# Row softmax of 512 MB on one core: the steady part of the unrolled kernel put into a hardware loop with register-based waits

## The chip, the cores and the metric

One core of a Trainium2 chip runs the kernel; the other cores idle. The metric is device time in microseconds (us), the median of several executions.

## The reference, cut to what matters

```python
logits: (16, 256, 32768) float32, temperature = 1.0
scaled = logits / temperature
scaled = scaled - scaled.max(axis=-1, keepdims=True)
e = np.exp(scaled)
out = e / e.sum(axis=-1, keepdims=True)          # float32
```

There are 4096 rows of 32768 numbers: 537 MB are read and 537 MB written. Each byte is moved once in each direction.

## The kernel before: the parts that matter

A row is split into two halves on two partitions, so a *group* is 64 rows on 128 partitions. A group is two *chunks* of 128 x 8192 numbers, 4 MiB each; there are 64 groups and 128 chunks. Six chunk buffers are used in turn. VectorE (DVE) takes each chunk's maximum, ScalarE (ACT) its exponentials and their sum. A few tiny instructions combine the two chunks and the two halves into factors; then DVE scales one half of each chunk and ACT the other. SyncE (SP) issues every load and store. Its main lines, shortened:

```python
xpool = ctx.enter_context(tc.tile_pool(name="x", bufs=6))
...
order = [("L", i) for i in range(6)] + [("S", 0)]         # L: load, S: compute and store
for i in range(1, n_chunks):
    order.append(("S", i))
    if i + 5 < n_chunks:
        order.append(("L", i + 5))                        # into the buffer of chunk i - 1
...
    if g > done:                                          # first chunk of a group
        exps(2 * g); exps(2 * g + 1); factors(g)
    scales(i); store(i)
```

All 128 chunks are unrolled. A scheduler orders DVE and ACT; loads and stores stay in program order.

## Time and profile before

| | before |
|---|---|
| time, median of 4 runs beside the changed kernel | 2494.67 us |
| DMA queue, share of the 16 engines' span | 99.9% |
| bytes moved, rate in the steady part | 1073.76 MB, 433 GB/s |
| DVE busy, ACT busy | 60%, 56% |
| instruction packets (they fetch the program while it runs) | 17 |

The queue row is the one to read: it is full. A busy engine at 60% has nothing to say about the time here. The lines themselves are in the prediction.

### The profile page before, as it was taken

To read this page: it belongs to the slowest core of one execution; us is meant where nothing else is said; L and a number is where in the kernel's file an instruction comes from. 1 tells how busy PE (TensorE), PEld (TensorE's weight loads), DVE (VectorE), ACT (ScalarE), POOL (GpSimd) and SP (SyncE) were. 2 spreads that over 40 slices of the span, in tenths; PEclk is the share of its full clock that TensorE was granted. 3 is DMA by queue.
4 is the path that set the end of the run, shared out by engine and by line. 5 is a ranking of instruction groups with operands and counts; after the bars stand their busy time and mean duration, and the time that the engine had idled before them with its cause. 6 is when DMAs were issued, how large, how long until landed. Compare 5 with 4: busy or idle time off the path is not lost.

```text
span 2493.8 us, 2234 instructions
## 1 busy us (share of the span) xinstructions
DVE 1487.4 (60%) x964; ACT 1405.0 (56%) x455; POOL 0.2 (0%) x4
## 2 busy tenths in 40 slices
DVE  7655565556655566555665566655666566655663
ACT  5665554655556555565555655555546555465553
POOL 0000000000000000000000000000000000000000
DMA  9999999999999999999999999999999999999998
GB/s 412 433 430 432 429 431 432 433 433 434 433 434 432 435 432 435 432 435 431 436 431 435 432 434 433 434 433 433 433 433 433 433 433 434 434 433 434 432 431 368
DMA packets 37745, 1073.90 MB, mean 431 GB/s; under 512 B 4192, under 2 KB 4192, under 8 KB 4192
## 3 DMA queue, kind: packets, MB, share of 16 engines
q1 hardware_dynamic: 37728, 1073.76, 99.9%
q14 instruction: 17, 0.14, 0.0%
HBM read 536.87 MB, written 536.87 MB: 431 GB/s over the span
## 4 chain that ended last, share of the span: by engine, by line
DMA 96%; SPq 1%; ACT 1%; DVE 1%; issue 1%; ACTq 0%
DMA out_dram<-xs 93%; DMA xs<-in_logits_dram 2%; SPq L64 1%; DVE nm L107 1%; ACT xs L163 1%; ACT xs L114 0%; ACTq L224 0%; SPq L75 0%; DVE f L150 0%; ACT ee L131 0%; DVE rS L149 0%; DVE Sh L87 0%; DVE ttj L138 0%; DVE Sh L84 0%; DVE Sh L138 0%
## 5 line engine op out<-in xcount | busy, mean ns | idle before, releaser
L114 ACT ACTIVATE xs<-xs,nm 128x8192 f32<-128x8192 f32 (+1 forms) x130 | 912.1, 7016 | 972.4 <-DVE nm L107 972.4
L107 DVE TENSOR_REDUCE nm<-xs 128x1 f32<-128x8192 f32 (+1 forms) x130 | 1111.6, 8551 | 527.3 <-DMA xs<-in_logits_dram 527.3
L163 ACT ACTIVATE xs<-xs,f 128x4096 f32<-128x4096 f32 (+1 forms) x130 | 468.1, 3648 | 71.4 <-DVE f L150 71.4
L160 DVE TENSOR_SCALAR xs<-xs,f 128x4096 f32<-128x4096 f32 (+1 forms) x130 | 295.7, 2318 | 3.7 <-DVE f L150 1.8
L138 DVE CUSTOM_DVE_ANT_0 ttj<-ee,ssum 128x2 f32<-128x2 f32 x64 | 10.3, 161 | 423.8 <-ACT ee L131 423.8
L114 ACT ACTIVATION_READ_ACCUMULATOR xs<-xs,nm 128x1 f32 x130 | 24.2, 186 | 0.0
L131 ACT ACTIVATE ee<-nm,nMh 128x2 f32<-128x2 f32 x64 | 17.9, 280 | 0.0
L150 DVE TENSOR_SCALAR f<-ee,rS 128x2 f32<-128x2 f32 x64 | 14.6, 229 | 2.2
L149 DVE RECIPROCAL rS<-Sh 128x1 f32<-128x1 f32 x64 | 10.5, 164 | 2.2
L87 DVE TENSOR_TENSOR nMh<-nMh 128x1 f32<-128x1 f32 x64 | 10.2, 160 | 2.2
L87 DVE TENSOR_TENSOR Sh<-Sh 128x1 f32<-128x1 f32 x64 | 10.2, 160 | 2.2
L129 DVE TENSOR_REDUCE nMh<-nm 128x1 f32<-128x2 f32 x64 | 9.9, 155 | 2.2
L84 DVE STREAM_SHUFFLE nMh<-nMh 128x1 f32<-128x1 f32 x64 | 9.7, 151 | 0.0
L84 DVE STREAM_SHUFFLE Sh<-Sh 128x1 f32<-128x1 f32 x64 | 9.7, 151 | 0.0
L114 ACT ACT_TABLE_LOAD x1 | 1.3, 1283 | 12.9 <-DMA xs<-in_logits_dram 12.9
L138 DVE DVE_READ_ACCUMULATOR2_ANT Sh<- 128x1 f32 x64 | 5.3, 84 | 0.0
L84 DVE LOAD_MASK_SELECT Sh<-Sh x64 | 0.9, 14 | 2.8
L84 DVE LOAD_MASK_SELECT nMh<-nMh x64 | 0.9, 14 | 2.7
L210 POOL MEMSET const-bfloat16-1.0<- 128x1 bf16 x1 | 0.1, 102 | 0.0
L210 POOL MEMSET const-uint8-127<- 128x1 uint8 x1 | 0.1, 102 | 0.0
L210 POOL MEMSET const-float32-0.0<- 128x1 f32 x1 | 0.1, 99 | 0.2 <-issue 0.2
L210 POOL MEMSET const-float32-1.0<- 128x1 f32 x1 | 0.1, 99 | 0.0
## 6 DMA issues: line engine op xcount, KB each, us to landing
out_dram<-xs SPq DMA_DIRECT2D x126, 4096.0 KB, 38.2
xs<-in_logits_dram SPq DMA_DIRECT2D x124, 4096.0 KB, 29.0
xs<-in_logits_dram SPq DMA_DIRECT2D x8, 2048.0 KB, 22.3
out_dram<-xs SPq DMA_DIRECT2D x4, 2048.0 KB, 26.7
```

Of the source, the lines that this page charges most:

```text
L64: nc.sync.dma_start(out=xs[:, s : s + n], in_=x[g * P : (g + 1) * P, c * CW + s : c * CW + s + n],)
L84: nc.vector.stream_shuffle(out=v[:, j + 1 : j + 2], in_=v[:, j : j + 1], mask=mask)
L87: nc.vector.tensor_tensor(out=v[:, j + 1 : j + 2], in0=v[:, j : j + 1], in1=v[:, j + 1 : j + 2], op=op,)
L107: nc.vector.tensor_reduce(out=nm[:, k : k + 1], in_=xs[:, s : s + n], axis=X, op=A.max, negate=True)
L114: nc.scalar.activation(out=xs[:, s : s + n], in_=xs[:, s : s + n], func=Exp, bias=nm[:, k : k + 1], scale=inv_t, accum_out=ssum[:, k : k + 1],
L129: nc.vector.tensor_reduce(out=nMh[:, 0:1], in_=nm, axis=X, op=A.min)
L131: nc.scalar.activation(out=ee, in_=nm, func=Exp, bias=nMh[:, n_rounds : n_rounds + 1], scale=-1.0,)
L138: nc.vector.tensor_tensor_reduce(out=ttj, in0=ee, in1=ssum, scale=1.0, scalar=0.0, op0=A.mult, op1=A.add, accum_out=Sh[:, 0:1],)
L149: nc.vector.reciprocal(out=rS, in_=Sh[:, n_rounds : n_rounds + 1])
L150: nc.vector.tensor_scalar_mul(out=f, in0=ee, scalar1=rS)
L160: nc.vector.tensor_scalar_mul(out=xs[:, s : s + cut], in0=xs[:, s : s + cut], scalar1=f[:, k : k + 1])
L163: nc.scalar.activation(out=xs[:, s + cut : s + n], in_=xs[:, s + cut : s + n], func=Copy, scale=f[:, k : k + 1],)
```

## The change

The intent is a short program: 114 of the 128 chunks are handled by 19 turns of a hardware loop whose body holds six chunks, one per buffer, 24 MiB loaded and 24 MiB stored in each turn. A loop of this kind needs no stop between turns: its semaphores are never reset, and every wait in the body compares with a register that is raised in each turn. For that the buffers become fixed tiles, and the engines run in the order in which the program names the work. Six chunks before the loop and eight after it stay unrolled.

```diff
-    xpool = ctx.enter_context(tc.tile_pool(name="x", bufs=_BUFS))
-    spool = ctx.enter_context(tc.tile_pool(name="stats", bufs=3))
+    pool = ctx.enter_context(tc.tile_pool(name="fixed", bufs=1))
+    buf = [pool.tile([P, CW], fp32, tag=f"x{b}", name=f"x{b}") for b in range(_BUFS)]
     ... (three fixed sets of the small tiles)
+    def rows(i, turn, per_turn):
+        g = i // C
+        if turn is None:
+            return slice(g * P, (g + 1) * P)
+        return bass.ds(turn * (per_turn // C * P) + g * P, P)     # address from a register
     ...
+    def step(i, turn=None, per_turn=0):
+        g, c = divmod(i, C)
+        end = turn is None and g == G - 1
+        if c == 0:
+            normalise(g, _END_PIECE if end else _PIECE)   # maxima, exponentials, factors, scaling
+        store(i, _END_DMA if end else CW, turn, per_turn)
+        j = i + _BUFS - 1
+        if i and j < n_chunks:
+            ... load(j, ...)
+    with tc.manual_schedule():
+        for i in range(_BUFS):
+            load(i, _END_DMA if i < C else CW)
+        for i in range(first):                                       # first = 6
+            step(i)
+        with tc.For_i(0, turns, 1, iteration_sync="reg_based") as turn:   # turns = 19
+            for i in range(first, first + per_turn):                  # per_turn = 6
+                step(i, turn, per_turn)
+        for i in range(first + turns * per_turn, n_chunks):           # chunks 120 to 127
+            step(i)
```

More of the change, by code (lines that the diff above doesn't have):

```diff
@@ L12 @@
 _PIECE = 8192
-_LAST_DMA = 4096
+_END_DMA = 4096
+_END_PIECE = 4096
 _DVE_SHARE = 0.5
+_SETS = 3
 @with_exitstack
@@ L45 @@
     n_rounds = _SPLIT.bit_length() - 1
-    xpool = ctx.enter_context(tc.tile_pool(name="x", bufs=_BUFS))
-    spool = ctx.enter_context(tc.tile_pool(name="stats", bufs=3))
-    slots = {}
-    stats = {}
+    K = W // min(_PIECE, _END_PIECE)
+    pool = ctx.enter_context(tc.tile_pool(name="fixed", bufs=1))
+    buf = [
+        pool.tile([P, CW], fp32, tag=f"x{b}", name=f"x{b}") for b in range(_BUFS)
+    ]
+    widths = dict(nm=K, ssum=K, ee=K, f=K, ttj=K, nMh=2, Sh=2, rS=1)
+    stat = [
+        {
+            k: pool.tile([P, w], fp32, tag=f"{k}{s}", name=f"{k}{s}")
+            for k, w in widths.items()
+        }
+        for s in range(_SETS)
+    ]
@@ L52, in spans @@
     def spans(total: int, step: int) -> list[tuple[int, int]]:
         return [(s, min(step, total - s)) for s in range(0, total, step)]
-    def piece(g: int) -> int:
-        return _PIECE if g < G - 1 else min(_PIECE, _LAST_DMA)
-    def load(i: int) -> None:
-        g, c = divmod(i, C)
-        xs = xpool.tile([P, CW], fp32, tag="x", name="xs")
-        slots[i] = xs
-        for s, n in spans(CW, _LAST_DMA if g in (0, G - 1) else CW):
-            tc.keep_in_program_order(
-                nc.sync.dma_start(
-                    out=xs[:, s : s + n],
-                    in_=x[g * P : (g + 1) * P, c * CW + s : c * CW + s + n],
-                )
-            )
@@ L70, in store, with rows @@
-    def store(i: int) -> None:
-        g, c = divmod(i, C)
-        xs = slots.pop(i)
-        for s, n in spans(CW, _LAST_DMA if g == G - 1 else CW):
-            tc.keep_in_program_order(
-                nc.sync.dma_start(
-                    out=o[g * P : (g + 1) * P, c * CW + s : c * CW + s + n],
-                    in_=xs[:, s : s + n],
-                )
+    def rows(i: int, turn, per_turn: int):
+        g = i // C
+        if turn is None:
+            return slice(g * P, (g + 1) * P)
+        return bass.ds(turn * (per_turn // C * P) + g * P, P)
@@ new lines, in load, with store @@
+    def load(i: int, step: int, turn=None, per_turn: int = 0) -> None:
+        c = i % C
+        for s, n in spans(CW, step):
+            nc.sync.dma_start(
+                out=buf[i % _BUFS][:, s : s + n],
+                in_=x[rows(i, turn, per_turn), c * CW + s : c * CW + s + n],
+            )
+    def store(i: int, step: int, turn=None, per_turn: int = 0) -> None:
+        c = i % C
+        for s, n in spans(CW, step):
+            nc.sync.dma_start(
+                out=o[rows(i, turn, per_turn), c * CW + s : c * CW + s + n],
+                in_=buf[i % _BUFS][:, s : s + n],
@@ L92, in combine, with pieces, normalise @@
             )
-    def exps(i: int) -> None:
-        g, c = divmod(i, C)
-        xs = slots[i]
-        ps = spans(CW, piece(g))
-        K = C * len(ps)
-        if c == 0:
-            stats[g] = tuple(
-                spool.tile([P, K], fp32, tag=f"{nm}{K}", name=nm)
-                for nm in ("nm", "ssum", "ee", "f", "ttj")
-            )
-        nm, ssum = stats[g][:2]
-        for j, (s, n) in enumerate(ps):
-            k = c * len(ps) + j
+    def pieces(g: int, step: int):
+        k = 0
+        for c in range(C):
+            xs = buf[(g * C + c) % _BUFS]
+            for s, n in spans(CW, step):
+                yield k, xs[:, s : s + n], n
+                k += 1
+    def normalise(g: int, step: int) -> None:
+        st = stat[g % _SETS]
+        K = W // step
+        nm, ssum, ee, f, ttj = (st[k][:, :K] for k in ("nm", "ssum", "ee", "f", "ttj"))
+        nMh, Sh, rS = st["nMh"], st["Sh"], st["rS"]
+        for k, xc, n in pieces(g, step):
             nc.vector.tensor_reduce(
-                out=nm[:, k : k + 1], in_=xs[:, s : s + n], axis=X, op=A.max, negate=True
+                out=nm[:, k : k + 1], in_=xc, axis=X, op=A.max, negate=True
             )
@@ L114, in exps @@
             nc.scalar.activation(
-                out=xs[:, s : s + n],
-                in_=xs[:, s : s + n],
+                out=xc,
+                in_=xc,
                 func=Exp,
@@ L121, in exps @@
             )
-    def factors(g: int) -> None:
-        nm, ssum, ee, f, ttj = stats[g]
-        nMh = spool.tile([P, 1 + n_rounds], fp32, tag="nMh", name="nMh")
-        Sh = spool.tile([P, 1 + n_rounds], fp32, tag="Sh", name="Sh")
-        rS = spool.tile([P, 1], fp32, tag="rS", name="rS")
-        with tc.high_priority():
-            nc.vector.tensor_reduce(out=nMh[:, 0:1], in_=nm, axis=X, op=A.min)
-            combine(nMh, A.min)
-            nc.scalar.activation(
-                out=ee,
-                in_=nm,
-                func=Exp,
-                bias=nMh[:, n_rounds : n_rounds + 1],
-                scale=-1.0,
-            )
-            nc.vector.tensor_tensor_reduce(
-                out=ttj,
-                in0=ee,
-                in1=ssum,
-                scale=1.0,
-                scalar=0.0,
-                op0=A.mult,
-                op1=A.add,
-                accum_out=Sh[:, 0:1],
-            )
-            combine(Sh, A.add)
-            nc.vector.reciprocal(out=rS, in_=Sh[:, n_rounds : n_rounds + 1])
-            nc.vector.tensor_scalar_mul(out=f, in0=ee, scalar1=rS)
@@ L152, in scales @@
-    def scales(i: int) -> None:
-        g, c = divmod(i, C)
-        xs = slots[i]
-        f = stats[g][3]
-        ps = spans(CW, piece(g))
-        for j, (s, n) in enumerate(ps):
-            k = c * len(ps) + j
+        nc.vector.tensor_reduce(out=nMh[:, 0:1], in_=nm, axis=X, op=A.min)
+        combine(nMh, A.min)
+        nc.scalar.activation(
+            out=ee, in_=nm, func=Exp, bias=nMh[:, n_rounds : n_rounds + 1], scale=-1.0
+        )
+        nc.vector.tensor_tensor_reduce(
+            out=ttj,
+            in0=ee,
+            in1=ssum,
+            scale=1.0,
+            scalar=0.0,
+            op0=A.mult,
+            op1=A.add,
+            accum_out=Sh[:, 0:1],
+        )
@@ L159, in scales @@
+        combine(Sh, A.add)
+        nc.vector.reciprocal(out=rS, in_=Sh[:, n_rounds : n_rounds + 1])
+        nc.vector.tensor_scalar_mul(out=f, in0=ee, scalar1=rS)
+        for k, xc, n in pieces(g, step):
             cut = int(n * _DVE_SHARE) // 512 * 512
             nc.vector.tensor_scalar_mul(
-                out=xs[:, s : s + cut], in0=xs[:, s : s + cut], scalar1=f[:, k : k + 1]
+                out=xc[:, :cut], in0=xc[:, :cut], scalar1=f[:, k : k + 1]
             )
             nc.scalar.activation(
-                out=xs[:, s + cut : s + n],
@@ L165, in scales @@
-                in_=xs[:, s + cut : s + n],
-                func=Copy,
-                scale=f[:, k : k + 1],
-            )
-    order = [("L", i) for i in range(min(_BUFS, n_chunks))] + [("S", 0)]
-    for i in range(1, n_chunks):
-        order.append(("S", i))
-        if i + _BUFS - 1 < n_chunks:
-            order.append(("L", i + _BUFS - 1))
-    nxt = 0
-    done = -1
-    loaded = 0
-    for kind, i in order:
-        if kind == "L":
-            load(i)
-            loaded = i + 1
-        else:
-            g = i // C
-            if g > done:
-                while nxt < (g + 1) * C:
-                    assert nxt < loaded
-                    exps(nxt)
-                    nxt += 1
-                factors(g)
-                done = g
-            scales(i)
-            store(i)
+                out=xc[:, cut:], in_=xc[:, cut:], func=Copy, scale=f[:, k : k + 1]
+            )
@@ new lines, in step @@
+    def step(i: int, turn=None, per_turn: int = 0) -> None:
+        g, c = divmod(i, C)
[5 more added lines that the diff above has]
+        if i and j < n_chunks:
+            end = turn is None and j // C == G - 1
+            load(j, _END_DMA if end else CW, turn, per_turn)
+    per_turn = 6
+    first = per_turn
+    turns = (n_chunks - (_BUFS - 1) - C - first) // per_turn
@@ L197 @@
+    assert turns > 0
+    with tc.manual_schedule():
[8 more added lines that the diff above has]
+            step(i)
 _INS = ['logits', 'temperature']
```

## The prediction

> **What bounds the kernel now.** I read the page from the top: busy shares, the 40 slices, the chain that ended last, then the waits of the DMA queue, then one stretch of the timeline. The first lines are these.
>
> ```profile
> span 2493.8 us, 2234 instructions
> DVE 1487.4 (60%) x964; ACT 1405.0 (56%) x455; POOL 0.2 (0%) x4
> ...
> GB/s 412 433 430 432 429 431 432 433 433 434 433 434 432 435 432 435 432 435 431 436 431 435 432 434 433 434 433 433 433 433 433 433 433 434 434 433 434 432 431 368
> ...
> q1 hardware_dynamic: 37728, 1073.76, 99.9%
> ...
> DMA 96%; SPq 1%; ACT 1%; DVE 1%; issue 1%; ACTq 0%
> ```
>
> Both compute engines are idle 40% of the time, the data queue's packets fill 99.9% of the 16 DMA engines' span, and the rate is flat at about 433 GB/s. The chain of waits is 96% DMA. So the time is bytes over rate: 1073.76 MB / 433.4 GB/s = 2477.5 us, and about 17 us remain for the slower start, and for the tail that shows as 368 in the last slice.
>
> The second question is how much work stands in the queue, because the change touches the waits there. The waits of the queue and the issue table show it.
>
> ```profile
> SPq L64 <- DMA out_dram<-xs: 2246.9, 122, 19.6
> ...
> out_dram<-xs SPq DMA_DIRECT2D x126, 4096.0 KB, 38.2
> xs<-in_logits_dram SPq DMA_DIRECT2D x124, 4096.0 KB, 29.0
> ```
>
> SP waits 122 times, 18.4 us on average, always before a load, for the store that frees its buffer. Call the store of chunk i S(i) and its load L(i). When S(i) has landed, L(i+6) goes out and S(i+2) directly after it. In the queue's timeline these refills stand 19.35 us apart, which is 8.39 MB (one load and one store of 4 MiB) at 433.4 GB/s. A single 4 MiB transfer therefore takes 9.67 us. The latencies fit a first-in first-out queue exactly: two transfers (19.35 us) still stand ahead, so the load lands after three (29.0) and the store after four (38.7, seen 38.2). Every refill finds 19.35 us of transfers in hand.
>
> The third question is how long one group of two chunks takes to compute when nothing overlaps it. This is from the timeline at 1978 us.
>
> ```profile
> 1978.30 8.69 DVE L107 TENSOR_REDUCE nm<-xs 128x1 f32<-128x8192 f32 x1 [8.31 <-DMA xs<-in_logits_dram]
> ...
> 1987.02 7.12 ACT L114 ACTIVATE xs<-xs,nm 128x8192 f32<-128x8192 f32 x1 [9.78 <-DVE nm L107]
> ...
> 1994.14 0.28 ACT L131 ACTIVATE ee<-nm,nMh 128x2 f32<-128x2 f32 x1
> ...
> 1995.24 0.23 DVE L150 TENSOR_SCALAR f<-ee,rS 128x2 f32<-128x2 f32 x1
> 1995.57 7.31 ACT L163 ACTIVATE xs<-xs,f 128x4096 f32<-128x4096 f32 x2 [1.15 <-DVE f L150]
> ```
>
> From the second reduction to the first half of the scaling it takes 1995.57 + 7.31/2 - 1978.30 = 20.9 us; with the first chunk's reduction before it, 20.9 + 8.7 = 29.6 us. A group's share of the queue is 38.7 us, so this is hidden today.
>
> **What the Trainium skill says.** "DMA: Bandwidth & Descriptors", section "Where 436 GB/s comes from", puts the ceiling of the 16 ports at 435.2 GB/s. The 433.4 measured is within half a per cent of it, so there is nothing to win in the steady part. The same page, "Anatomy of one DMA", gives about 2 us fixed per transfer, mostly the receipt of the last bytes, and says that waits happen on the issuing sequencer. The trace agrees: the first 4 MiB is issued from 0.73 us and released its reduction at 12.89, so 12.16 - 9.67 = 2.5 us beyond the transfer. "Runtime: NRT & Kernel Launch", section "Instruction fetch mechanics", warns that a taken branch to a target outside the two pages held makes the engine fetch before it goes on. No trace of the kernel before can show that; it has no loop.
>
> **The change part by part.** I compared the built orders of instructions and semaphores of both kernels.
>
> *Bytes.* None change: the same 264 transfers in the same order of loads and stores. Term: 0.
>
> *Engines in program order.* The scheduler had put the next group's first reduction between this group's exponentials and its factors; now the factors and scaling come first. Per group DVE has 2 x 8.7 + 2 x 2.3 + about 1.5 = 23.5 us of work in 38.7 us. It stays hidden. Term: 0.
>
> *Register arithmetic and the branch.* The loop is 19 turns of 6 chunks (chunks 6 to 119); 6 chunks before it and 8 after it are unrolled. No engine meets a barrier at the end of a turn: each adds to its wait registers and branches. SP branches just after a load, when it would wait some 19 us for the next landing anyway. Term: 0.
>
> *A new wait inside the loop.* With addresses from a register the framework no longer sees that two stores go to different rows. In the loop every store waits until the store before it has landed, the first store of a turn included. So S(i+1) and L(i+6) go out when S(i) lands, and the queue then holds one load, 9.67 us, not 19.35. Less the 2.5 us fixed cost, some 7 us are in hand, and the order of transfers is the same. If no DMA engine runs dry, the term is 0; a store's latency in the table should drop from 38 to about 19 us and a load's stay at 29.
>
> *The end of the loop.* Here something is added once. After the last turn SP waits for every transfer of the loop, then all engines meet at a barrier; only then do DVE and ACT start on chunks 120 and 121, though both landed long before. S(120) is next in SP's order, and L(125) stands behind it although its buffer is free. So the DMA engines idle for: fixed cost of the last landing and of the first new issue 2.5 us (above), barrier about 0.7 us (SP's wait for the others at the start was 0.7 us), compute 29.6 us, issue 0.4 us. Sum **33.2 us**. Nothing can hide it: the queue is the bound, and time lost there is not won back. Following the eight chunks after it by the same durations, S(122) and S(124) are ready before the queue is empty, and the store of chunk 126 comes within about 1 us of its emptying. Term: +33.2 + 1 = 34.
>
> *Instruction fetches.* The 2234 instructions before came in through 17 packets of the instruction queue. The refill intervals are 19.35 us except for one of 20.16, 0.8 us longer, every 16 chunks, and a handful of longer ones in the first 20 chunks; all this excess is about 11 us. A loop may remove part of it. Term, a guess: -3.
>
> Sum: 2494.9 + 34 - 3 = 2526 us, 1.2% longer.
>
> **The rivals.** *A.* The store-to-store wait starves the queue. Against it: 7 us are in hand. For it: the 16 DMA engines do not end together (in the last 14 us the rate falls step by step, so some finish some 10 us before the last), and with a shorter queue the early ones will idle. As long as the slowest never runs dry it alone sets the pace. But if the pace stays at the 19.6 us of the first 20 chunks rather than 19.35, 114 chunks x 0.28 us add 32 us: 2558 us. If every refill exposed the 2.5 us, 114 x 2.5 = 285 us: 2810 us; the queue's arithmetic speaks strongly against that.
>
> *B.* Every turn stalls on an instruction fetch or a hidden drain. The program shows no drain in the body, and the branch has some 19 us of slack; 5 us exposed per turn would be 95 us: 2621 us.
>
> *C.* The end of the loop is hidden after all, because instructions behind the barrier are short or loads run ahead. Then 2490 to 2495 us. Against it: the barrier stands in every engine's order, and the 29.6 us of compute cannot start before it.
>
> **Range and chances.** 2527 us is the sum of the one-time gap and a small gain. Low end 2508: a gap of 25 us and most of the 11 us of excess gone. High end 2553: the gap plus a good part of rival A. The 2% line lies at 2544.8; the gap alone does not cross it, so it takes rival A or B to cross. I give that 16%. Faster by over 2% would need 1073.76 MB in 2445 - 17 = 2428 us, 442 GB/s, above anything the slices show: 1%.
>
> **What would show each step.** In the changed profile: one hole of about 33 us in the DMA row near 2385 us (the loads of chunks 126 and 127 wait today for the store of chunk 121 until 2415 us), with DVE's first reduction after it released by the barrier and not by a load; otherwise 433 GB/s per slice; store latency near 19 us and load latency near 29; SP's waits on a store's landing moved from the loads to the stores; fewer instruction packets. The prediction is wrong if the slices in the loop lie below 430 GB/s (A), if a dip comes every 116 us (B), or if no hole is there (C).

## The result, and the profile after

The changed kernel takes **2531.05 us** (median of 4 runs, 2530.07 to 2532.89) against 2494.67 us (4 runs). The ratio is 1.0147, with a 95% interval of 1.0129 to 1.0165. Ratios here are the mean time of one kernel's runs over the mean of the other's in the same rounds, so not quite the ratio of the medians. The profiled executions have spans of 2529.0 and 2493.8 us: **35.2 us** are to be found.

The page of the changed kernel, the lines that answer to those shown of before:

```profile
span 2529.0 us, 4017 instructions
DVE 1486.7 (59%) x964; ACT 1405.5 (56%) x455; POOL 0.2 (0%) x4
...
GB/s 415 431 399 421 433 431 430 431 434 433 433 432 434 433 433 433 434 433 434 432 434 433 434 432 434 433 434 432 434 433 434 432 434 433 434 432 434 300 314 416
...
q1 hardware_dynamic: 37728, 1073.76, 98.6%
q14 instruction: 2, 0.02, 0.0%
...
DVE 3%; ACT 1%; ACTq 0%; issue 0%
...
out_dram<-x SPq DMA_DIRECT2D x126, 4096.0 KB, 19.2
x<-in_logits_dram SPq DMA_DIRECT2D x124, 4096.0 KB, 28.3
```

The bytes and the compute are those of before. Most of the 1800 instructions more are register arithmetic, counted in every turn. Slices 5 to 37 are as fast as before. Two places are not: slices 3 and 4 (399, 421), and slices 38 and 39 (300, 314). The chain that ended last names only some 5% of the span: it could be followed back to a barrier and no further, so here it does not say what bounds the kernel.

The second place is where the loop ends. The timeline there (start, duration, engine, line, operation; L83 is the store, L75 the load, L115 the maximum, L122 the exponential, L153 ACT's scaling):

```profile
2358.41 0.34 SPq L83 DMA_DIRECT2D out_dram<-x  x1
2358.97 0.35 SPq L75 DMA_DIRECT2D x<-in_logits_dram  x1
2388.08 17.28 DVE L115 TENSOR_REDUCE nm<-x 128x1 f32<-128x8192 f32 x2 [75.64 <-PEq L213]
...
2405.39 7.12 ACT L122 ACTIVATE x<-x,nm 128x8192 f32<-128x8192 f32 x1 [1.38 <-DVE nm L115]
...
2413.94 7.31 ACT L153 ACTIVATE x<-x,f 128x4096 f32<-128x4096 f32 x2 [1.15 <-DVE f L147]
2417.67 0.34 SPq L83 DMA_DIRECT2D out_dram<-x  x1
```

SP issues the loop's last load at 2358.97 us. The waits of the queue tell that it then stands for that load:

```profile
SPq L178 <- DMA x<-in_logits_dram: 27.6, 1, 27.6
```

So the loop is drained at about 2387 us. DVE starts at 2388.08 us, after 75.64 us of idleness; "PEq" is only the last engine to come to the barrier, not work of TensorE. The compute up to the next store takes 2417.67 - 2388.08 = 29.6 us. What the DMA engines did meanwhile (stretches of 10 us, the first of 20; the last two numbers are the share of the 16 DMA engines and GB/s):

```profile
2360.00:2380.00 20.00, 0.00 (x0) 0.00 (x0) 0.00 (x0) 1.00 1.00 433
2380.00:2390.00 10.00, 1.92 (x1) 0.00 (x0) 0.00 (x0) 1.00 0.31 134
2390.00:2400.00 10.00, 10.00 (x2) 3.20 (x1) 0.00 (x0) 1.00 0.00 0
2400.00:2410.00 10.00, 5.82 (x5) 8.62 (x3) 0.00 (x0) 1.00 0.00 0
2410.00:2420.00 10.00, 6.99 (x10) 8.85 (x5) 0.00 (x0) 1.00 0.25 105
```

That is the hole of the prediction. The queue was empty while DVE and ACT worked, and before that DVE and ACT had idled while the queue worked.

The first place is where the loop is entered:

```profile
141.25 0.34 SPq L75 DMA_DIRECT2D x<-in_logits_dram  x1
142.02 17.28 DVE L115 TENSOR_REDUCE nm<-x 128x1 f32<-128x8192 f32 x2 [36.84 <-SPq L178]
...
171.67 0.35 SPq L83 DMA_DIRECT2D out_dram<-x  x1
```

DVE had finished the group before at 105 us, and chunk 6, its next, should have been there (loaded from 72.05 us; a load takes 28.3 us). It waits 36.84 us for "SPq L178", the line of the loop itself, and goes on just after SP has issued its last load ahead of the loop. The reason is not in the trace; this is how I read the built program: the waits in the loop use semaphores of the loop's own, and each engine gives its own semaphores their starting count where it stands in its program ahead of the loop. The counts for the loads are SP's, and SP comes to that place only when it has issued the unrolled part's last load, at 141.25 us. So the store of chunk 6 goes out at 171.67 us, when three queued transfers (29.0 us) have run dry. The DMA engines from 164 to 176 us, in slices of 0.3 us (each digit is their busy share in tenths):

```profile
DMA  2997299729992020002000000000900092009500
```

A ledger follows from the queue's timelines. It gives the time at which a load is issued in the changed kernel, less the time of the same load in the kernel before (in the last row, the spans):

| load of chunk | changed less before, us | run with the compute ahead (below) less before, us |
|---|---|---|
| 10 (before the loop is entered) | +0.7 | +0.9 |
| 15 | +5.4 | +2.0 |
| 25 | +6.4 | +0.4 |
| 65 | +4.5 | -1.3 |
| 124 (last of the loop) | +1.7 | -4.2 |
| end | +35.2 | 0.0 |

The entry costs 4.7 us by load 15 and 5.7 us by load 25; from there to load 124 the changed kernel gains 4.7 us on the kernel before; the exit costs 33.5 us. The gain is in the refill intervals. Before, from load 25 on, seven late ones of 20.16 us stand among those of 19.35. Each of the seven holds one instruction packet; the other ten of the 17 packets go with no late interval after load 25. In the changed kernel there are 2 packets, none between 110 and 2440 us, and no such interval. So the late intervals go with fetches; that the fetch makes them late is not shown. From load 28 to 124 the sum of what exceeds 19.355 us falls from 4.7 to 0.7 us.

### The profile page after: what moved, and what is told of

The parts are those of the page before. It is cut to its first block, busy times and chain, and to the rows that moved or that the text cites. A ratio compares the mean times of both kernels' runs of the same rounds, so it can differ in the third digit from the quotient of the medians.

```text
span 2529.0 us, 4017 instructions
## 1 busy us (share of the span) xinstructions
DVE 1486.7 (59%) x964; ACT 1405.5 (56%) x455; POOL 0.2 (0%) x4
## 5 line engine op out<-in xcount | busy, mean ns | idle before, releaser
L122 ACT ACTIVATE x<-x,nm 128x8192 f32<-128x8192 f32 (+1 forms) x130 | 912.1, 7016 | 1017.5 <-DVE nm L115 678.2
L115 DVE TENSOR_REDUCE nm<-x 128x1 f32<-128x8192 f32 (+1 forms) x130 | 1110.5, 8550 | 559.8 <-DMA x<-in_logits_dram 447.4
L153 ACT ACTIVATE x<-x,f 128x4096 f32<-128x4096 f32 (+1 forms) x130 | 468.1, 3649 | 73.4 <-DVE f L147 73.4
L150 DVE TENSOR_SCALAR x<-x,f 128x4096 f32<-128x4096 f32 (+1 forms) x130 | 295.7, 2318 | 2.3
L122 ACT ACTIVATION_READ_ACCUMULATOR x<-x,nm 128x1 f32 x130 | 24.2, 186 | 0.0
## 6 DMA issues: line engine op xcount, KB each, us to landing
out_dram<-x SPq DMA_DIRECT2D x126, 4096.0 KB, 19.2
x<-in_logits_dram SPq DMA_DIRECT2D x124, 4096.0 KB, 28.3
```

What stands on the lines that cost most here:

```text
L115: nc.vector.tensor_reduce(out=nm[:, k : k + 1], in_=xc, axis=X, op=A.max, negate=True)
L122: nc.scalar.activation(out=xc, in_=xc, func=Exp, bias=nm[:, k : k + 1], scale=inv_t, accum_out=ssum[:, k : k + 1],)
L150: nc.vector.tensor_scalar_mul(out=xc[:, :cut], in0=xc[:, :cut], scalar1=f[:, k : k + 1])
L153: nc.scalar.activation(out=xc[:, cut:], in_=xc[:, cut:], func=Copy, scale=f[:, k : k + 1])
```

## The experiments

My theory was: one hole at the exit, made of drain and compute; one small hole at the entry; a small gain from fetches; and nothing from the turns or from the stores that wait for one another. The rivals were a cost of each turn, a cost of the store-to-store wait, and a cost of program order. Twelve kernels ran, all with correct results. The kernel before, run beside them, had medians of 2494.2 to 2494.6 us.

**Program order and fixed buffers without a loop.**

```diff
-        for i in range(first):
-            step(i)
-        with tc.For_i(...) as turn: ...
-        for i in range(first + turns * per_turn, n_chunks):
+        for i in range(n_chunks):
             step(i)
```

> The change without its loop: fixed buffers, engines in program order, all 128 chunks unrolled. Theory (the loss is one gap where the loop is left, one small gap where it is entered, less instruction fetches that the loop saves): none of these three is here, so 2494 to 2496 us, within 3 us of the kernel before, with 433 GB/s in every slice, refills of 19.35 us with the 0.8 us longer ones still there, and no hole. Rival (program order itself or the fixed buffers cost time, because factors and scaling now stand before the next reduction): 2505 us or more.

Measured: 2494.92 us, ratio 1.0004 (0.999 to 1.0017). There are 17 instruction packets again, and the intervals of 20.15 to 20.17 us are back. Program order and fixed buffers cost nothing; the 36 us need the loop or what comes with it.

**Compute a group ahead of the loop's boundary.** The computing of group g+1 moves from just before its own stores to just after the stores of group g.

```diff
-        if c == 0:
-            normalise(g, _END_PIECE if end else _PIECE)
         store(i, _END_DMA if end else CW, turn, per_turn)
         ... load(j, ...)
+        if c == C - 1 and g + 1 < G:
+            last = turn is None and g + 1 == G - 1
+            normalise(g + 1, _END_PIECE if last else _PIECE)
 ...
+        normalise(0, _PIECE)
         for i in range(first):
             step(i)
```

> The changed kernel with one thing moved: a group is computed after the stores of the group before it, not directly before its own stores, so chunks 120 and 121 are computed before the loop is left, and 6 and 7 before it is entered. Store-to-store waits, turns, barrier and drain stay as they were. Theory: the hole at the exit shrinks from 33 us by the 29.6 us of compute to about 3.6 us (fixed cost 2.5, barrier 0.7, issue 0.4), the hole at the entry (about 4 us, from DVE idle 36.8 us until SP reached the loop) is gone, the saved fetches stay: 2490 to 2495 us, as fast as the kernel before or a little faster. Rival (the loss is in the turns, or in the wait of a store for the store before it): 2520 us or more, as both are still there.

Measured: 2495.39 us, ratio 1.0007 (0.9994 to 1.0021). The turns, the store-to-store waits, the drain and the barrier are all still there, and the loss is gone. The timeline at the exit:

```profile
2353.14 0.35 SPq L75 DMA_DIRECT2D x<-in_logits_dram  x1
2382.29 17.28 DVE L115 TENSOR_REDUCE nm<-x 128x1 f32<-128x8192 f32 x2 [36.95 <-PEq L215]
2382.31 0.34 SPq L83 DMA_DIRECT2D out_dram<-x  x1
```

DVE and SP leave the barrier together, and the store goes out at once. Three refills over the exit take 62.1 us in place of 3 x 19.355 = 58.1: the hole is 4.1 us, 3.6 expected. It was 33.6 us in the changed kernel by the same count (91.6 - 58.1). The ledger shows the version 4.2 us ahead of the kernel before when the exit comes; it gives all of that back and ends level. It ties with the kernel before and beats the changed kernel by 35 us.

**Enter the loop at chunk 0.**

```diff
-        if i and j < n_chunks:
+        if j < n_chunks:
 ...
-    first = per_turn
+    first = 0
 ...
-        for i in range(_BUFS):
+        for i in range(_BUFS - 1):
             load(i, ...)
```

> The changed kernel with the six unrolled chunks ahead of the loop taken into it: 20 turns from chunk 0, five loads ahead. SP then reaches the loop with nothing to wait for, before DVE has data. Theory: DVE no longer idles for SP at the loop's entry, so the entry hole of about 4 us is gone and only the exit hole of 33 us is left: 2525 to 2528 us against some 2531 for the changed kernel. Rival (the entry costs nothing; the 5.3 us seen between the refills of chunks 5 and 10 come from elsewhere, as from the first turns of any loop): 2530 to 2532 us.

Measured: 2525.63 us, ratio 1.0127; the third slice is 429 GB/s where it was 399. SP has nothing to wait for ahead of this loop, and DVE's wait for SP is gone from the list of waits. So the entry was worth 2531.05 - 2525.63 = 5.4 us, by medians of different rounds, and the exit is left. (The loads before the loop are one fewer, too; the run with the compute ahead, which removes the entry's wait in another way, agrees: by load 25 it stands only 0.4 us behind.)

**Two loops of 10 and 9 turns.**

```diff
-        with tc.For_i(0, turns, 1, iteration_sync="reg_based") as turn:
+        with tc.For_i(0, 10, 1, iteration_sync="reg_based") as turn:
             ...
+        with tc.For_i(10, turns, 1, iteration_sync="reg_based") as turn:
+            ... (the same body)
```

> The changed kernel with its 19 turns split into two loops of 10 and 9 turns, one directly after the other. Theory: one more exit with its drain, barrier and 29.6 us of compute: a second hole of about 33 us in the middle, 2562 to 2568 us; the second loop's entry adds nothing of its own, as SP has nothing left to wait for there. Rival (cost per turn or per store): the count of turns and stores is the same, so 2531 us.

Measured: 2575.11 us, ratio 1.0329. A second exit costs 44 us, not the 33 expected. The direction is the theory's, the size was a miss. Some 2.4 us of it lie outside the profiled span (time less span is 4.2 to 4.4 us here, 1.9 us in the changed kernel). The five runs spread more than in any other kernel (2574.28 to 2593.97). The profiled one was the slowest, and in it the refills of the first loop stayed between 19.2 and 20.7 us for hundreds of microseconds. Why that run never settled I do not know.

**Half the turns.**

```diff
-    first = per_turn
+    first = 60
```

> The changed kernel with 60 chunks unrolled ahead of the loop and 10 turns in place of 19. Theory (one exit, one entry, whatever the turns): the exit hole is unchanged at 33 us, the entry hole stays, fewer instruction fetches are saved: 2530 to 2534 us. Rival (a cost of each turn or of each store in the loop): the loss of 36 us falls in proportion to the turns, to about 19 us: 2514 us.

Measured: 2539.31 us, ratio 1.0179. The rival of a cost per turn (2514 us) falls: with 10 turns in place of 19 the loss grew. But the time is 5 us above my range. DVE's wait for SP at the entry was 46.7 us here, and the three refills over it took 64.1 us for 58.1, so 6 us as in the changed kernel (64.2). New was that the 20 refills after it were slow again: their sum exceeds 20 x 19.355 by 5.7 us. The start of most runs shows the same: 5.9 us over the 20 refills from load 8 in the kernel before, 5.5 to 6.4 us in the runs with no loss at the entry and no stop there; only 3.6 us in the loop from chunk 0. This led to the last four runs.

**A full stop between turns.**

```diff
-        with tc.For_i(0, turns, 1, iteration_sync="reg_based") as turn:
+        with tc.For_i(0, turns, 1, iteration_sync="barrier") as turn:
```

> The changed kernel with the plain kind of loop: all engines stop between turns to reset the semaphores. Theory: what stands once at the exit now stands at every turn: 18 more holes of about 33 us (drain, barrier, 29.6 us of compute), some 600 us: 3080 to 3160 us. Rival (a stop between turns is a few microseconds, as only the branch and two barriers are added): 2531 + 18 x 4 = 2600 us.

Measured: 3161.04 us, ratio 1.2667. The page's row of slices, each of 79 us, shows a hole in nearly every second one:

```profile
GB/s 418 430 432 259 401 250 423 253 421 245 424 242 431 238 432 244 431 240 420 254 383 286 351 318 319 351 286 384 253 418 252 424 246 427 241 426 242 431 241 420
```

(3161.04 - 2531.05) / 18 = 35.0 us for each further stop: drain and compute, 19 times. This is what register-based waits save in this kernel.

**Stores that do not wait for one another.** The output is named through six views that are declared disjoint.

```diff
+    views = dram_disjoint_views(o, _BUFS)
 ...
-                out=o[rows(i, turn, per_turn), c * CW + s : c * CW + s + n],
+                out=views[i % _BUFS][rows(i, turn, per_turn), c * CW + s : c * CW + s + n],
```

> The changed kernel with its output named as six views that the framework takes to be disjoint, one for each buffer, so that a store in the loop no longer waits for the store before it. The stores go to different rows, so nothing is unsafe. Theory: the queue holds two transfers more than it needs either way; the latency of a store in the issue table goes back from 19 to about 38 us, and the time stays within 4 us of the changed kernel, 2527 to 2533 us. If the deeper queue also bridges the entry, where S(6) was 30 us late, a few us may come back. Rival (the store-to-store wait is a part of the loss): 2500 to 2520 us.

Measured: 2530.86 us, ratio 1.0147, the changed kernel's to the last digit. The issue table shows that the wait was really gone:

```profile
out_dram<-x SPq DMA_DIRECT2D x126, 4096.0 KB, 37.9
x<-in_logits_dram SPq DMA_DIRECT2D x124, 4096.0 KB, 29.0
```

The store's 37.9 us is back from 19.2. A store then waits longer in the queue instead of in front of it; nothing else changes. The deeper queue did not bridge the entry either.

**Both moves together** (the compute ahead, and the six views).

> Both moves together: a group computed ahead of the loop's boundary, and six disjoint views of the output. Theory: nothing is left for the views to bring, 2490 to 2495 us, within 2 us of the run with the computing ahead alone. Rival (a shorter queue costs some tenths of a per cent in the loop): 3 to 8 us faster than that run.

Measured: 2497.20 us, ratio 1.0009 (0.9995 to 1.0022). It is not faster than the compute ahead alone. Its median is 1.8 us higher; the two are of different rounds and chips and I read nothing into that.

**One stop without any loop, at three places.** The unrolled kernel in program order, with one stop of all engines. SP waits until all has landed; then DVE and ACT go on.

```diff
         for i in range(n_chunks):
+            if i == 60:                                   # 120 and 12 in the other two
+                tc.strict_bb_all_engine_barrier()
             step(i)
```

> No loop at all: the unrolled kernel in program order, with one stop of all engines before chunk 60, where SP waits until every transfer has landed and only then DVE and ACT go on. It is what the loop's exit does, alone and in the middle of the run. Theory one (a stop costs its hole, and nothing else): 2494.9 + 33 = 2528 us. Theory two, formed after the runs with half the turns and with two loops came out 5 to 10 us above what was expected (a stop also costs about 20 slower refills after it, 19.65 us for 19.35, as at the start of every run): 2528 + 6 = 2534 us, with those refills to be seen. Rival (the loss needs the loop): 2495 us.

> The same stop before chunk 120, where the changed kernel has its exit. Only 11 transfers follow, so theory two has no room for 20 slow refills. Theory one and theory two: 2527 to 2530 us. If theory two is right this is 4 to 7 us less than the stop before chunk 60; if theory one is right they are equal. The changed kernel at 2531 us should be within 4 us of it.

> The same stop before chunk 12, while the refills are still slow from the start of the run. Theory two: the slow stretch of the start is cut off and begins again, so only a part of it, some 2 to 4 us, is paid twice: 2530 to 2532 us, between the stops before chunks 120 and 60. Theory one: 2528 us.

Measured: 2532.37 us before chunk 60 (ratio 1.0154), 2528.88 us before chunk 120 (1.0138), 2530.19 us before chunk 12 (1.0144). The slices of the first of them:

```profile
GB/s 414 431 431 431 434 431 431 435 433 432 434 434 432 433 434 434 433 433 435 170 422 428 433 433 433 432 433 434 434 431 435 433 433 432 434 433 434 433 431 395
```

SP's loads around that stop (loads of chunks 64 to 67; other lines left out):

```profile
1193.29 0.34 SPq L75 DMA_DIRECT2D x<-in_logits_dram  x1
...
1252.49 0.38 SPq L75 DMA_DIRECT2D x<-in_logits_dram  x1
...
1264.22 0.34 SPq L75 DMA_DIRECT2D x<-in_logits_dram  x1
...
1285.49 0.34 SPq L75 DMA_DIRECT2D x<-in_logits_dram  x1
```

So the loss needs no loop: a single stop makes it. The stop before chunk 120 costs 2528.88 - 2494.92 = 34.0 us, as much as the changed kernel's exit. Before chunk 60 it costs 3.5 us more, and the slices after the hole (422, 428) show where: three refills over the hole (1285.49 - 1193.29 = 92.2 us) exceed their share of 58.1 by 34.1 us, and the eight after them by 3.2 us. The slowest run with the stop before chunk 120 (2529.17) lies below the fastest with the stop before chunk 60 (2531.55). Theory two holds in kind. Its size of 6 us was too large for this place. The stop before chunk 12 came out between the other two, in its expected range, but theory one's 2528 us is only 2 us away: it says little alone.

**The stop before chunk 60, with chunks 60 and 61 computed ahead of it.**

> The stop before chunk 60 with chunks 60 and 61 computed ahead of it. Theory: the 29.6 us of compute leave the hole, 3.6 us stay (fixed cost, hand-over, issue). Theory one: 2495 + 3.6 = 2498.5 us. Theory two (the slow refills follow any stop that lets the DMA engines run empty, however short): 2498.5 + 6 = 2504 us. Rival (a stop is paid by its drain and not by the compute behind it): 2525 us or more.

Measured: 2502.23 us, ratio 1.0032 (1.0019 to 1.0044). The hole shrinks to 4.1 us (62.2 us for three refills), and the 16 refills after it exceed theirs by another 4.1 us. The slow stretch thus follows even a hole of 4 us. By the same count of 16 refills the hole of 34 us was followed by 3.6 us. So the stretch does not grow with the hole; these are single profiled executions, and why it comes is not shown.

## Why the prediction was right, point by point

- *What bounds the kernel.* Right. The queue is the bound, and lost queue time is not won back: in the stop without a loop, 34 us of hole gave 34 us of time.
- *Same bytes, program order, terms of 0.* Right; the kernel in program order without a loop took 2494.92 us.
- *The new store-to-store wait, term 0.* Right, and by the mechanism told: store latency 19.2 us, load 28.3, and the time unchanged when the wait was taken away. The pace did settle at 19.36 us with the shorter queue.
- *Turns without cost.* Right: with 10 turns in place of 19 the time did not fall.
- *The end of the loop, 33.2 us.* Right: 33.6 us by refills, of which compute is 29.6 us in the timeline; computing ahead left 4.1 us. DVE began 1.2 us after the drain where 0.7 was put for the barrier.
- *"Here something is added once."* This step failed. Something is added at the entry too: 5 to 6 us (5.4 by the loop from chunk 0), because DVE waits for SP there, as I read it for the loop's starting counts. The order of semaphores that I had read contains it; I followed only the exit.
- *Instruction fetches, -3, "a guess".* Right in sign, too small in size: 4.7 us between loads 25 and 124; the cause is as the prediction guessed only in that the late intervals go with fetches.
- *The tail, +1.* Not seen: the exit and all after it make 33.5 us together.
- *The sum.* Its terms give 2525.9 us; the 2527 of the range is 1 us more than they do. Against the 31.2 us of the terms 35.2 us came: 5.7 at the entry and 0.7 ahead of it were left out, the gain was 1.7 larger than put and the exit with its tail 0.7 smaller. That the sum came within 5 us owes a little to luck: 6.4 us were left out, and the smaller misses gave 2.4 of them back.
- *The signs of being wrong.* One of them came true to the letter: two slices of the loop, 399 and 421, lie below the 430 GB/s that were to convict rival A. They are the entry: in the loop from chunk 0 the same slices are 429 and 430, with the store-to-store wait still there. Rival A's 0.28 us a chunk does not follow from its own 19.6 - 19.35 = 0.25, which changes nothing.

## What to carry to other kernels

A loop without stops between its turns still has a stop where it is left, and its semaphores a start where it is entered. In a kernel bound by its transfers, ask at both places what the first transfer behind it needs, and have that computed on the near side. Here that one move was worth 35 us, while depth of queue, number of turns and order of engines were worth nothing; and it brought the loop level with the unrolled kernel, not ahead of it.

## What the Trainium skill lacked or had wrong

- No page has that the rate is lower for a while after the DMA engines have run empty. At the start of the kernel before, 20 refills exceed 20 x 19.355 us by 5.9 us. After a stop in mid-run it was 3.2 us over 8 refills or, with the compute ahead, 4.1 us over 16; after a late loop entry 5.7 us over 20. The cause is open. One observation: in the kernel before, the rate falls over the last 12 us, and in the changed kernel, after its late drain, only over the last 3 us (the last slice is 368 GB/s there and 416 here).
- "Runtime: NRT & Kernel Launch", section "Instruction fetch mechanics", calls the cost of going on to the next block of instructions "mostly hidden". With a full queue a small cost may show: seven refills are 0.8 us longer than the others, and each holds one instruction packet; ten further packets go with none. The stall that it warns of at a taken branch had no occasion in 19 turns: no packet came between 110 and 2440 us.
- "DMA: Bandwidth & Descriptors", section "Where 436 GB/s comes from", says that for transfers between HBM and SBUF the limit of about 358 GB/s binds. For one core alone this is wrong, as the same page's table of measured loads has it too (425 GB/s): here one core, loading and storing at once, held 433 GB/s for some 2400 us.
- The same page, "Anatomy of one DMA", fits its fixed cost of about 2 us to transfers that GpSimd issues; the page has no fit for those that SP issues, as here. The prediction cited it without that limit; its 2.5 us came from the trace. The runs show 2.5 us beyond the transfer on the first load, and 4.1 us for a drained hole with nothing to compute, barrier and issue included.
